# Two layers of a hybrid mixer and FFN on one core: the S5 matrices of layer 1 built beside another product, with one load per block

## The chip, the cores and the metric

One core of a Trainium2 chip. The metric is the device time of one execution in microseconds; a run counts as the time of its slowest core, which here is the only one. Five engines work from five instruction queues, each in its own order: PE (matmuls), DVE, ACT, POOL and SP (which here only starts DMAs). An instruction that waits holds back everything behind it in its queue, and a DMA is started by an instruction in the queue of SP, ACT or POOL.

## The reference

For an activation of 256 tokens by 2048 channels, two layers each compute a norm, a wide projection, three mixers (block-sparse attention, an S5 state-space mixer, a gated delta rule), an output projection, and a convolutional FFN of width 5504:

```python
for l in range(DEPTH):                                   # DEPTH = 2
    h = rmsnorm(x, attn_norm[l])
    (q, kc, vc, ks, vs, kw, vw, nsa_gates, u, qkv, z, a, b) = jnp.split(h @ w_in[l], split_points, axis=-1)
    y_a = nsa_mixer(...); y_b = s5_mixer(u, ...); y_c = gdn_mixer(...)
    x = x + concat([rmsnorm(y_a), rmsnorm(y_b), y_c]) @ w_out[l]
    x = x + conv_ffn(rmsnorm(x, ffn_norm[l]), ffn_w_in[l], ffn_conv[l], ffn_conv_b[l], ffn_w_out[l])
```

The S5 mixer is a complex linear recurrence per group. The kernel runs it four tokens at a time, and so needs, for each layer, tables of powers of the recurrence's factor and four blocks of small matrices that hold B and C multiplied by its powers. These depend on parameters alone, not on x.

## The kernel before, in words

All large products go through `product` (lines 353 to 367) or its token-major twin. A product reads its weights in units: `load` (L338) brings one unit of up to 1024 columns per partition (512 KB) into `raw` by a DMA of SP; `weight` splits it in two by `split_to`, ACT copying the high part `whi` (L327) and DVE subtracting it from `raw` to give the low part `wlo` (L328); PE then issues three matmuls per 128 rows (high by high, high by low, low by high; L295). `raw`, `whi` and `wlo` have three buffers each, so the split runs at most three units ahead of PE.

The FFN (`ffn`, from L451) runs in two halves of 22 and 21 column blocks f. In each half the first product makes, for every f, a gate and an up column block (two products of 48 matmuls, evacuated by DVE at L436, followed by a convolution on ACT and DVE at L441 and L443, a silu, a multiplication and another split into gh and gl). Then the second product makes 16 column blocks c of the output from the 22 (or 21) gh, gl: 66 (63) matmuls per c in three weight units, one addition per c on DVE (L484).

The S5 matrices of layer 1 are made during the FFN of layer 0, those of layer 0 at the start of its own mixers, by the same two functions:
- `s5_tables` (L970): some 75 tiny DVE instructions on 128x16 tiles, two sines on ACT, two powers on POOL, then POOL doubles a table `tb` six times (L1044 to L1049).
- `s5_blocks(ct)`, ct = 0 to 3 (L1054): four DMAs of 64 KB from ACT's queue bring B into `s5b` (L1066) and C straight into the block's matrix tile `s5V` (L1067); POOL multiplies B by a coefficient and then three times by the factor (helper `times`, L1075 to L1077); PE transposes eight 128x128 pieces of `s5V` (L1091), ACT copies them (`s5g`, L1094), PE multiplies small pieces of `s5V` into W, ACT copies W (L1109), and SP writes everything to a DRAM tensor `parts`, in five DMAs. `s5V`, `s5b` and `s5g` have one buffer each: the next block's first write to `s5V` waits until PE, ACT and SP have read the last one.

Order: the program is traced in source order, and a list scheduler then puts each engine's instructions in the order in which its own model of time finds them ready, with source order as priority. Nothing moves at run time. `issue_after(i)` adds an edge: every instruction traced inside it, on the engine of i, stands behind i in that engine's queue. In the kernel before, the tables of layer 1 are traced after the first product of the FFN's first half, behind the POOL power of the FFN's norm, and block ct at f = 24, 28, 32, 36 of the second half's first product.

Of the kernel before, what the change touches and what calls it, by code (L numbers as in the profile page):

```python
# [6 lines left out]
F32 = mybir.dt.float32  # L7
F32R = mybir.dt.float32r
BF16 = mybir.dt.bfloat16
AF = mybir.ActivationFunctionType  # L10
OP = mybir.AluOpType
# [25 lines left out]
SUB = 4  # L37
TABLES = (24, 28, 32, 36)
NC4 = T // SUB
# [220 lines left out]
def _s5_mats(inp, l):  # L260
    out = np.zeros((4, 2, 64, 16, 2, 16), np.float32)
    for i, nm in enumerate(("b_re", "b_im", "c_re", "c_im")):
# [3 lines left out]
        for gp in range(2):  # L266
            out[i, gp, :, :, gp] = a[:, :, gp]
    return np.ascontiguousarray(out.reshape(4, 128, 512).transpose(1, 0, 2))

# [3 lines left out]
class _K:  # L273
# [51 lines left out]
    def split_to(self, hi, lo, src, engine=None):  # L325

        self.nc.scalar.activation(out=hi, in_=src, func=AF.Copy)  # L327
        (engine or self.nc.vector).tensor_tensor(lo, src, hi.bitcast(F32), OP.subtract)  # L328

# [117 lines left out]
    def ffn(self, last):  # L447
        nc, tc = self.nc, self.tc
# [3 lines left out]
        with tc.tile_pool(name="ffn", bufs=2, reuse_waits="tile") as fp, tc.tile_pool(name="skewg", bufs=1) as skew, \  # L452
                tc.tile_pool(name="ffg", bufs=23, reuse_waits="tile") as gp:
            skew.tile([128, 16], F32, name="skewg")
            for hf, fs in enumerate(HALVES):
                gh, gl = {}, {}
                for f in fs:
                    if hf and not last and f in TABLES:
                        self.l += 1
                        self.s5_blocks(TABLES.index(f))  # L460
                        self.l -= 1
                    out = []
# [12 lines left out]
                if hf:  # L475
                    self.acc = self.squares()
                elif not last:
                    self.l += 1
                    with tc.issue_after(self.pow):
                        self.s5_tables()  # L480
                    self.l -= 1
                for c in range(16):
                    ps = self.product(("fo", hf, c), fs, gh, gl)
                    nc.vector.tensor_tensor(self.x[c], ps, self.x[c], OP.add)  # L484
                    if hf and not last:
                        self.add_square(self.acc, c)
# [566 lines left out]

    def s5_blocks(self, ct):  # L1054

        nc, s5 = self.nc, self.s5v[1]
        gt = self.either(12).tensor_tensor
        src = self.ap[f"s5m{self.l}"].rearrange("p m (t q h) -> p m t q h", t=4, q=4)[:, :, ct]

# [3 lines left out]
                               ap=[V.ap[0], [256, 8], [128 + 32 * (2 * m - 3), 2], [1, 32]])  # L1063
        sb = s5.tile([128, 4, 2, 32], F32, name="s5b", tag="s5b")
        for r in range(2):
            nc.scalar.dma_start(sb[:, :, r, :], src[:, r])  # L1066
            nc.scalar.dma_start(v6[:, :, r, 1, 0, :], src[:, 2 + r])  # L1067

        def times(out, x, by, n):
# [445 lines left out]
```

## Time and profile before

| | us |
|---|---|
| median of three runs | 2512.08 |
| the three runs | 2519.9, 2479.57, 2512.08 |
| the profiled execution, its own time | 2475.74 |
| its span, first to last instruction | 2473.9 |
| mean granted TensorE clock in it | 0.985 of full |

All durations below come from the profiled execution; its span leaves 1.8 us outside. A busy time is the sum over an engine's instructions in a stretch; "[x <-Y]" behind a row is the idle time of that engine just before the row and what ended it.

### The profile page before, as it was taken

The page shows a single profiled execution, that of the slowest core. Times are in us where ns is not written, and L with a number is a line of the kernel's source. Part 1 is how long each engine was busy: PE and PEld are TensorE (multiplying, and loading weights), DVE is VectorE, ACT ScalarE, POOL GpSimd, SP SyncE. Part 2 cuts the span into 40 slices and gives each one's busy share as a digit, 9 for nine tenths or more (in the row PEclk, how much of TensorE's full clock was granted, in tenths as well). Part 3 has the DMA queues.
Part 4 walks back from the last instruction along what each step waited for, and adds up shares of the span by engine and source line. Part 5 has one row for each costly group of instructions (what it writes and reads, how often), then busy time and mean ns, then how long its engine had stood idle before and what let it go on. Part 6 is the DMA issues. An engine that isn't in the chain of part 4 may idle for free.

```text
span 2473.9 us, 53497 instructions
## 1 busy us (share of the span) xinstructions
PE 2417.8 (98%) x21822; PEld 2338.8 (95%) x21822; DVE 1773.5 (72%) x3058; ACT 1224.7 (50%) x1911; POOL 362.8 (15%) x470
## 2 busy tenths in 40 slices
PE   8889999999999999999999999999999999999999
PEld 8879898899999999999999999988999999999999
DVE  8778766778777557787667887577877765677754
ACT  5444444564555445555545444445655544455543
POOL 7753013007100003410000021210000000000000
PEclk9999998999999999999999999989999999999999
DMA  7667455364666666666776644643655556555565
GB/s 247 174 196 206 149 183 175 98 186 159 195 195 193 191 197 206 207 208 193 213 234 202 220 138 150 216 139 99 194 195 193 193 192 196 194 194 196 193 204 175
DMA packets 206086, 463.16 MB, mean 187 GB/s; under 512 B 47600, under 2 KB 95120, under 8 KB 205840
## 3 DMA queue, kind: packets, MB, share of 16 engines
q1 hardware_dynamic: 187344, 456.13, 58.5%
q10 hardware_dynamic: 17984, 2.62, 0.6%
q8 instruction: 171, 2.80, 0.5%
q0 software_dynamic: 512, 0.98, 0.1%
q14 instruction: 75, 0.61, 0.1%
HBM read 437.96 MB, written 18.63 MB: 185 GB/s over the span
## 4 chain that ended last, share of the span: by engine, by line
PE 84%; DVE 5%; POOL 4%; DMA 3%; issue 2%; ACT 1%; ACTq 0%; SPq 0%; DVEq 0%; POOLq 0%
PE gps L295 75%; PE mpss L295 3%; PE mpsh L295 3%; PE mpsm L295 2%; DVE wlo L328 2%; POOL s5tmp L1075 2%; DMA parts<-s5g 1%; DMA raw<-w 1%; ACT whi L327 1%; DMA s5V<-s5m 1%; DVE xl L388 1%; PE mpss L907 0%; POOL s5V L1077 0%; DVE cva L443 0%; POOL s5V L1076 0%
## 5 line engine op out<-in xcount | busy, mean ns | idle before, releaser
L327 ACT ACTIVATE whi<-raw 128x1024 fp32r<-128x1024 f32 (+5 forms) x824 | 826.0, 1004 | 957.7 <-PE gps L295 804.7
L328 DVE TENSOR_TENSOR wlo<-raw,whi 128x1024 fp32r<-128x1024 f32 (+5 forms) x824 | 970.4, 1178 | 451.0 <-ACT whi L327 438.8
L295 PE MATMUL gps<-xh,wlo 128*128 128x256 f32 x3904 | 1090.6, 279 | 12.9 <-DVE wlo L328 12.7
L295 PE MATMUL gps<-xh,whi 128*128 128x256 f32 x3904 | 1090.2, 279 | 8.3 <-ACT whi L327 5.9
L295 PE MATMUL gps<-xl,whi 128*128 128x256 f32 x3904 | 1088.6, 279 | 0.0
L295 PEld LDWEIGHTS gps<-xh,wlo 128*128 128x128 f32 x3904 | 738.6, 189 | 19.2 <-DVE wlo L328 15.9
L295 PEld LDWEIGHTS gps<-xh,whi 128*128 128x128 f32 x3904 | 737.9, 189 | 12.4 <-ACT whi L327 6.7
L295 PEld LDWEIGHTS gps<-xl,whi 128*128 128x128 f32 x3904 | 738.4, 189 | 3.8 <-issue 3.0
L295 PE MATMUL gps<-gl,whi 128*128 128x256 f32 x1376 | 379.6, 276 | 0.0
L295 PE MATMUL gps<-gh,wlo 128*128 128x256 f32 x1376 | 379.6, 276 | 0.0
L295 PE MATMUL gps<-gh,whi 128*128 128x256 f32 x1376 | 379.1, 276 | 0.0
L295 PEld LDWEIGHTS gps<-gh,wlo 128*128 128x128 f32 x1376 | 258.3, 188 | 0.0
L295 PEld LDWEIGHTS gps<-gl,whi 128*128 128x128 f32 x1376 | 258.3, 188 | 0.0
L295 PEld LDWEIGHTS gps<-gh,whi 128*128 128x128 f32 x1376 | 258.0, 188 | 0.0
L295 PE MATMUL gps<-mh,wlo 128*128 128x256 f32 x512 | 148.0, 291 | 2.3 <-DVE wlo L328 2.3
L295 PE MATMUL gps<-mh,whi 128*128 128x256 f32 x512 | 148.3, 293 | 0.0
L295 PE MATMUL gps<-ml,whi 128*128 128x256 f32 x512 | 147.9, 291 | 0.0
L436 DVE TENSOR_TENSOR cvp<-gps,R 128x256 f32<-128x256 f32 x220 | 92.6, 422 | 59.9 <-PE gps L295 59.1
L295 PEld LDWEIGHTS gps<-mh,wlo 128*128 128x128 f32 x512 | 100.9, 198 | 4.2 <-DVE wlo L328 2.7
L295 PEld LDWEIGHTS gps<-ml,whi 128*128 128x128 f32 x512 | 101.2, 198 | 0.1
L295 PEld LDWEIGHTS gps<-mh,whi 128*128 128x128 f32 x512 | 100.7, 198 | 0.2
L443 DVE SCALAR_TENSOR_TENSOR cvag<-cvp,parf,cvag 128x255 f32<-128x255 f32 (+1 forms) x172 | 89.6, 521 | 5.1 <-ACT cvag L441 2.2
(358 smaller groups left out, 2534.6 us busy)
## 6 DMA issues: line engine op xcount, KB each, us to landing
raw<-w SPq DMA_DIRECT2D x572, 512.0 KB, 4.1
raw<-w SPq DMA_DIRECT2D x192, 448.0 KB, 3.9
raw<-w SPq DMA_DIRECT2D x32, 320.0 KB, 3.1
raw<-w SPq DMA_DIRECT2D x32, 256.0 KB, 2.6
s5go<-parts SPq DMA_DIRECT2D x32, 192.0 KB, 4.4
parts<-s5V SPq DMA_DIRECT2D x16, 256.0 KB, 2.9
parts<-s5g SPq DMA_DIRECT2D x16, 256.0 KB, 3.7
s5gi<-parts SPq DMA_DIRECT2D x32, 128.0 KB, 3.6
```

The costliest lines, as they stand in the source:

```text
L295: self.nc.tensor.matmul(out, lhsT, rhs, start=start, stop=stop)
L327: self.nc.scalar.activation(out=hi, in_=src, func=AF.Copy)
L328: (engine or self.nc.vector).tensor_tensor(lo, src, hi.bitcast(F32), OP.subtract)
L388: nc.vector.scalar_tensor_tensor(o, self.x[k], self.p(gain, k), h.bitcast(F32), OP.mult, OP.subtract)
L436: nc.vector.tensor_tensor(p, ps, R, OP.mult)
L443: nc.vector.scalar_tensor_tensor(a[:, j:], p[:, :T - j], tap(n - 1 - j), a[:, j:], OP.mult, OP.add)
L1075: gt(t[i], x, w.to_broadcast(shape), OP.mult)
```

## The change

The tables of layer 1 are traced in the second product of the FFN's first half, ahead of c = 1, their DVE instructions behind the low part of the last weight unit traced so far. Blocks 0 to 3 follow ahead of c = 4, 7, 10 and 13 of the same product. The host now lays the S5 inputs out so that one block's B and C stand side by side (a contiguous 1 KB of each per partition); one DMA per block brings both (256 KB) into `s5b`, which is larger and has two buffers, and for layer 1 that DMA stands in ACT's queue behind the last copy of a high part traced so far. C then goes from `s5b` into `s5V` by a copy on POOL, at the head of the block. Both layers use the new load and copy; layer 0's tables and blocks stay where they are in the source.

```diff
--- before.py
+++ after.py
@@ -35,7 +35,7 @@
 )
 BANKS = (3, 2, 2, 1)
 SUB = 4
-TABLES = (24, 28, 32, 36)
+TABLES = (1, 4, 7, 10, 13)
 NC4 = T // SUB
 BASE = 16
 SKEW = 192
@@ -265,7 +265,8 @@
         a = a.reshape(64, 16, 2, 16)
         for gp in range(2):
             out[i, gp, :, :, gp] = a[:, :, gp]
-    return np.ascontiguousarray(out.reshape(4, 128, 512).transpose(1, 0, 2))
+
+    return np.ascontiguousarray(out.reshape(2, 2, 128, 16, 32).transpose(2, 0, 3, 1, 4)).reshape(128, 2, 1024)
 
 
 
@@ -324,8 +325,10 @@
 
     def split_to(self, hi, lo, src, engine=None):
 
-        self.nc.scalar.activation(out=hi, in_=src, func=AF.Copy)
-        (engine or self.nc.vector).tensor_tensor(lo, src, hi.bitcast(F32), OP.subtract)
+        self.copied = self.nc.scalar.activation(out=hi, in_=src, func=AF.Copy).ins
+        i = (engine or self.nc.vector).tensor_tensor(lo, src, hi.bitcast(F32), OP.subtract).ins
+        if engine is None:
+            self.split = i
 
 
     def load(self, key, pool=None):
@@ -455,10 +458,6 @@
             for hf, fs in enumerate(HALVES):
                 gh, gl = {}, {}
                 for f in fs:
-                    if hf and not last and f in TABLES:
-                        self.l += 1
-                        self.s5_blocks(TABLES.index(f))
-                        self.l -= 1
                     out = []
                     for s, j in (("g", f), ("u", NF + f)):
                         ps = first or self.product(("f" + s, f), range(KT), xh, xl)
@@ -474,12 +473,15 @@
                     self.split_to(gh[f], gl[f], g)
                 if hf:
                     self.acc = self.squares()
-                elif not last:
-                    self.l += 1
-                    with tc.issue_after(self.pow):
-                        self.s5_tables()
-                    self.l -= 1
                 for c in range(16):
+                    if not hf and not last and c in TABLES:
+                        self.l += 1
+                        if c == TABLES[0]:
+                            with tc.issue_after(self.split):
+                                self.s5_tables()
+                        else:
+                            self.s5_blocks(TABLES.index(c) - 1, self.copied)
+                        self.l -= 1
                     ps = self.product(("fo", hf, c), fs, gh, gl)
                     nc.vector.tensor_tensor(self.x[c], ps, self.x[c], OP.add)
                     if hf and not last:
@@ -1051,21 +1053,25 @@
             if n < NC4:
                 pc, pq = square(pc, pq)
 
-    def s5_blocks(self, ct):
+    def s5_blocks(self, ct, after=None):
 
         nc, s5 = self.nc, self.s5v[1]
         gt = self.either(12).tensor_tensor
-        src = self.ap[f"s5m{self.l}"].rearrange("p m (t q h) -> p m t q h", t=4, q=4)[:, :, ct]
+        bc = s5.tile([128, 2, 4, 2, 32], F32, name="s5b", tag="s5b", bufs=2)
+        load = lambda: nc.scalar.dma_start(bc.rearrange("p m q r h -> p m (q r h)"),
+                                           self.ap[f"s5m{self.l}"][:, :, 256 * ct:256 * ct + 256])
+        if after is None:
+            load()
+        else:
+            with self.tc.issue_after(after):
+                load()
 
         V = s5.tile([128, 4 * 512], F32, name="s5V", tag="s5V")
         v6 = V.rearrange("p (q r b s h) -> p q r b s h", q=4, r=2, b=2, s=4)
         at = lambda m: bass.AP(tensor=V.tensor, offset=V.offset + 32 * (3 - m),
                                ap=[V.ap[0], [256, 8], [128 + 32 * (2 * m - 3), 2], [1, 32]])
-        sb = s5.tile([128, 4, 2, 32], F32, name="s5b", tag="s5b")
-        for r in range(2):
-            nc.scalar.dma_start(sb[:, :, r, :], src[:, r])
-            nc.scalar.dma_start(v6[:, :, r, 1, 0, :], src[:, 2 + r])
-
+        sb = bc[:, 0]
+        self.either(12).tensor_copy(v6[:, :, :, 1, 0, :], bc[:, 1])
         def times(out, x, by, n):
 
             shape = [128, 8, n, 32]
```

ACT's queue before, in the FFN's first product of the first half (layer 0), about twenty weight units into it; `s5b<-s5m` is a load for layer 1:

```order
L1066 DMA s5b<-s5m 128x4x32 x2
L327 ACTIVATE whi<-raw 128x1024
L441 ACTIVATE cvag<-cvp,parf 128x256
L327 ACTIVATE whi<-raw 128x1024
L469 ACTIVATE sg<-cvag 128x256
L327 ACTIVATE whi<-raw 128x1024
L441 ACTIVATE cvau<-cvp,parf 128x256
L327 ACTIVATE whi<-raw 128x1024
L327 ACTIVATE gh<-gg 128x256
L327 ACTIVATE whi<-raw 128x1024
L441 ACTIVATE cvag<-cvp,parf 128x256
L1066 DMA s5b<-s5m 128x4x32
```

ACT's queue of the change, in the second product of that half; the copies of high parts that stand between the two loads are those of c = 4 to 6:

```order
L1061 DMA s5b<-s5m 128x2x256
L328 ACTIVATE whi<-raw 128x1024
L328 ACTIVATE whi<-raw 128x896 x2
L328 ACTIVATE whi<-raw 128x1024
L328 ACTIVATE whi<-raw 128x896 x2
L328 ACTIVATE whi<-raw 128x1024
L328 ACTIVATE whi<-raw 128x896 x2
L1061 DMA s5b<-s5m 128x2x256
L1100 ACTIVATE s5g<-mpss 128x512
```

The loads have left the first product; in the second they go into a buffer that is free, and between them stand only copies of high parts.

PE's queue before, at block 0 of layer 1, in the second half's first product at f = 24:

```order
L295 MATMUL gps<-xh,whi 128x256
L295 MATMUL gps<-xl,whi 128x256
L295 MATMUL gps<-xh,wlo 128x256
L1091 MATMUL mpss<-cst,s5V 128x128 x8
L295 MATMUL gps<-xh,whi 128x256
```

PE's queue of the change, at the same transposes:

```order
L296 MATMUL gps<-gh,whi 128x256
L1097 MATMUL mpss<-cst,s5V 128x128 x4
L296 MATMUL gps<-gl,whi 128x256
L296 MATMUL gps<-gh,wlo 128x256
L1097 MATMUL mpss<-cst,s5V 128x128 x4
```

Here 418 of the second product's 1056 matmuls stand ahead of the first transposes (6.33 c). Those of blocks 1, 2 and 3 stand at 8.76, 11.35 and 14.52 c, and the small matmuls into W, the last PE reads of `s5V`, 0.33 c behind the transposes.

DVE's queue before, in the tables, in the first product; `s5ps` and `s5pc` hold the factors of `tb`'s doublings, and POOL's first doubling waits for the pair that these rows make:

```order
L328 TENSOR_TENSOR wlo<-raw,whi 128x1024
L1021 TENSOR_TENSOR s5pc_10470<-s5pc_10470,s5t 128x16
L443 SCALAR_TENSOR_TENSOR cvag<-cvp,parf,cvag 128x255
L1018 TENSOR_TENSOR s5t<-s5ps_10471 128x16
L1019 TENSOR_TENSOR s5t_10469<-s5pc_10470,s5ps_10471 128x16
L1020 TENSOR_TENSOR s5pc_10472<-s5pc_10470 128x16
L443 SCALAR_TENSOR_TENSOR cvag<-cvp,parf,cvag 128x254
L1022 TENSOR_SCALAR s5ps_10473<-s5t_10469 128x16
```

DVE's queue of the change, at the same steps; the low part that leads is that of the first weight unit of c = 2:

```order
L329 TENSOR_TENSOR wlo<-raw,whi 128x1024
L1012 COPY s5c_10545<-s5ci 128x32
L1023 TENSOR_TENSOR s5pc_10548<-s5pc_10548,s5t 128x16
L1020 TENSOR_TENSOR s5t<-s5ps_10549 128x16
L1021 TENSOR_TENSOR s5t_10547<-s5pc_10548,s5ps_10549 128x16
L1022 TENSOR_TENSOR s5pc_10550<-s5pc_10548 128x16
L1024 TENSOR_SCALAR s5ps_10551<-s5t_10547 128x16
```

The same steps have moved from between convolutions to behind a split for the second product.

## Rows read from the trace of the kernel before

**Rows 1.** The page: part 1's engine totals, and part 4's chain by engine.

```profile
PE 2417.8 (98%) x21822; PEld 2338.8 (95%) x21822; DVE 1773.5 (72%) x3058; ACT 1224.7 (50%) x1911; POOL 362.8 (15%) x470
...
PE 84%; DVE 5%; POOL 4%; DMA 3%; issue 2%; ACT 1%; ACTq 0%; SPq 0%; DVEq 0%; POOLq 0%
```

**Rows 2.** Windows, FFN of layer 0: length; busy PE, PEld, DVE, ACT, POOL; clock; DMA.

```profile
581.34:630.79 49.45, 43.20 (x338) 42.20 (x337) 42.38 (x64) 20.94 (x29) 42.95 (x50) 0.93 0.54 161
630.79:641.70 10.91, 10.91 (x98) 10.91 (x98) 8.27 (x12) 5.79 (x9) 0.00 (x0) 1.00 0.68 210
836.86:844.34 7.48, 7.48 (x68) 7.48 (x67) 3.83 (x4) 2.97 (x4) 0.00 (x0) 1.00 0.58 198
940.91:949.00 8.09, 8.09 (x106) 7.81 (x105) 4.61 (x8) 4.89 (x10) 2.45 (x3) 1.00 0.77 217
940.91:1091.92 151.01, 148.40 (x1426) 146.17 (x1425) 120.46 (x151) 82.69 (x121) 56.65 (x52) 1.00 0.68 208
...
605.00:610.00 5.00, 3.25 (x15) 3.05 (x16) 4.09 (x6) 3.67 (x6) 4.90 (x5) 0.68 0.43 115
```

**Rows 3.** Timeline of ACT: start, length, instruction, idle time before it. ACTq is its queue.

```profile
603.69 0.98 ACTq L1066 DMA_DIRECT2D s5b<-s5m  x2
604.79 1.06 ACT L327 ACTIVATE whi<-raw 128x1024 fp32r<-128x1024 f32 x1 [4.91 <-PE gps L295]
...
624.02 1.06 ACT L327 ACTIVATE whi<-raw 128x1024 fp32r<-128x1024 f32 x1 [5.35 <-POOL s5tmp L1075]
...
966.11 0.60 ACT L441 ACTIVATE cvag<-cvp,parf 128x256 f32<-128x256 f32 x1 [4.25 <-POOL s5tmp L1075]
```

**Rows 4.** Timeline of PE behind those two ACT waits.

```profile
605.90 0.39 PE L295 MATMUL gps<-xh,whi 128*128 128x256 f32 x1 [1.65 <-ACT whi L327]
...
625.13 0.38 PE L295 MATMUL gps<-xh,whi 128*128 128x256 f32 x1 [2.85 <-ACT whi L327]
```

**Rows 5.** Timelines of POOL and of DVE: tables and block 0 of layer 1.

```profile
579.33 0.22 POOL L1045 TENSOR_TENSOR s5tmp<-tb,s5ps 128x16 f32<-128x16 f32 x1 [12.22 <-DVE s5pc L1021]
...
602.29 1.37 POOL L1075 TENSOR_TENSOR s5tmp<-s5b,s5c 128x256 f32<-128x256 f32 x2
...
604.84 1.27 POOL L1049 TENSOR_TENSOR tb<-tb,s5tmp 128x512 f32<-128x512 f32 x1
...
614.33 3.09 POOL L1075 TENSOR_TENSOR s5tmp<-s5V,s5l 128x512 f32<-128x512 f32 x2
...
622.31 1.18 POOL L1075 TENSOR_TENSOR s5tmp<-s5b,s5c 128x256 f32<-128x256 f32 x2
623.46 0.72 POOL L1076 TENSOR_TENSOR s5V<-s5tmp 128x256 f32<-128x256 f32 x1
...
579.07 0.16 DVE L1021 TENSOR_TENSOR s5pc<-s5pc,s5t 128x16 f32<-128x16 f32 x1
```

**Rows 6.** Groups by line and shape: POOL up to 170 us, then the FFN's second product.

```profile
L1310 POOL COPY ub<-cst 32x256 f32<-32x256 f32 x1 | 0.7, 736 | 0.0
L1098 POOL MEMSET s5W<- 128x512 f32 x4 | 2.1, 522 | 1.5 <-DMA parts<-s5W 1.5
...
L328 DVE TENSOR_TENSOR wlo<-raw,whi 128x1024 fp32r<-128x1024 f32 x24 | 29.4, 1225 | 31.6 <-ACT whi L327 31.5
L327 ACT ACTIVATE whi<-raw 128x1024 fp32r<-128x1024 f32 x24 | 25.5, 1063 | 38.2 <-PE gps L295 38.2
```

**Rows 7.** Timelines of the start of layer 0: PE, then ACT, then POOL.

```profile
88.81 1.11 PE L1091 MATMUL mpss<-cst,s5V 128*128 128x128 f32 x4 [3.49 <-POOL s5V L1076]
...
118.64 1.11 PE L1091 MATMUL mpss<-cst,s5V 128*128 128x128 f32 x4 [1.42 <-POOL s5V L1076]
...
68.94 0.51 ACT L439 ACTIVATE cva<-cvp,parm 128x256 f32<-128x256 f32 x1 [2.26 <-issue]
...
102.15 3.02 POOL L1075 TENSOR_TENSOR s5tmp<-s5V,s5l 128x512 f32<-128x512 f32 x2 [3.83 <-DMA s5V<-s5m]
107.54 2.04 POOL L1075 TENSOR_TENSOR s5tmp<-s5V,s5l 128x512 f32<-128x512 f32 x2
```

## The prediction, made before the run

> **What bounds the kernel now.** I read the page first. PE is busy 98% of the span and the chain that ended last runs 84% through it [rows 1], so a change can win only where PE stands still or runs below its rate, and loses wherever it adds a wait to PE. Next come the windows, to see what PE's rate is. With POOL idle, two products of the FFN of layer 0 take 10.91 us, 5.455 each, and one column block c of the second product takes 7.48 us, with PE busy throughout and its clock at 1.00 [rows 2]. These are the rates against which stretches with POOL at work are held.
>
> The first such stretch, 581.34 to 630.79, holds POOL's tables and block 0 for layer 1 beside seven products. Seven take 38.2 us at the rate; the stretch has 49.45 [rows 2]. So 11.3 us are lost, of which PE's idle time is 49.45 - 43.20 = 6.25. The timelines name the cause. ACT stands still for 4.91 and 5.35 us with a load of `s5b` at the head of its queue, until POOL has read the one buffer [rows 3]; behind the load wait copies of high parts, and PE waits for those, 1.65 and 2.85 us before the copy alone [rows 4]. The remaining 5.05 us beyond the idle time, 2.5 per stall, are slow running after it: at 605 to 610 the granted clock is 0.68 of full, a mean of the levels 1.2 and 2.4 GHz, right behind an idle PE [rows 2].
>
> The second stretch, 940.91 to 1091.92, holds the PE part of block 0 and all of blocks 1 to 3 beside 25 products: 136.4 us at the rate. The PE work of one block shows alone in 940.91 to 949.00: 8.09 - 5.455 = 2.6 us; four make 10.5. The stretch took 151.01, so 4.1 us are lost [rows 2], again with a load waiting in ACT's queue, 4.25 us behind POOL's reading of the B before it [rows 3].
>
> **The change, part by part.** *Loads of layer 1.* They leave both stretches, and what they meet in the second product is a free buffer and copies around them. The ACT stalls on `s5b` go, and DVE, 86% busy in the first stretch (42.38 of 49.45) with POOL's instructions beside it, is relieved [rows 2]. I take back all that was lost: 11.3 + 4.1 = 15.4 us. The upper bound is that sum; the lower is the second stall's part alone, some 5 us, if the rest came from the tables' DVE work rather than the loads. I take the upper end because each loss ends in a row that names the load's release [rows 3, 4].
>
> *Tables and blocks in the second product.* PE's own 2.6 us per block move and cost the same. DVE is only 51% busy there (3.83 of 7.48) [rows 2], so I cost the 75 small DVE instructions at nothing: the split is up to three units ahead. Without that cover they would cost up to what the first stretch lost beyond the load stalls.
>
> The term that decides is a new wait: PE's transposes of block 0 stand 6.33 c into the product, that is 47.3 us behind its start, and PE stops there until POOL has the matrices. When has it? POOL's doublings need factors that DVE makes behind the split of the first unit of c = 2. Its buffer comes free when PE ends the first unit of c = 1: 7.48 + 24 of 66 matmuls, 2.72, makes 10.2 us. Add the copy, 1.06, the split, 1.23 [rows 6], and six small DVE instructions of at most 0.16 [rows 5], 0.8 with their overlap: POOL starts at 13.3. In the trace the tables then take 26.8 us (579.33 to 606.11), and block 0 from there to the end of its last L1076, without the 1.18 us for the next block's B, 16.9 [rows 5]. Those are beside a DVE 86% busy. The same pair of L1075 took 3.09 us there and 2.04 us in a calmer place [rows 5, 7], a ratio of 0.66. So the bounds are 17.7 and 26.8 for the tables, 11.2 and 16.9 for the block. For a DVE 51% busy I go that share of the way between them: 23.1 and 14.6. The new copy of C on POOL is of a kind that the trace has not; the nearest row, a COPY of the same columns, took 0.74 us [rows 6]. Its bounds are 0.5, the memset row [rows 6], and 1.4, a pair of half-size multiplications (602.29) [rows 5]. POOL is ready at 13.3 + 23.1 + 0.7 + 14.6 = 51.7, and PE waits 4.4 us. With all low bounds (42.9) it waits nothing, with all high ones (58.4) 11.1. To a wait belongs the slow running behind it, 2.5 us as above. Behind the waiting PE stand further matmuls, ACT's copy of the transposes with the next high parts, and SP's writes with the next raw loads; all wait for the same event, so nothing is added.
>
> Blocks 1 to 3: `s5V` comes free 0.33 c and 2.6 us behind the transposes, 5.1 us; POOL then needs copy, memset and block, 0.7 + 0.5 + 14.6. That loop of 20.9 us stands against 2.43 c + 2.6 = 20.8 on PE's side for block 1, 22.0 for block 2, 26.3 for block 3. I take 0.1 us.
>
> The Trainium skill, SBUF — State Buffer, section Who interferes with whom, has a DVE instruction with two SBUF inputs hold off a GpSimd instruction that reads SBUF, for its whole length. The L1075 pairs, 3.09 against 2.04 us, agree in kind. By that rule taken strictly, three splits of some 1.15 us per c would leave POOL 54% of the time, and tables and block would take longer than in the first stretch, not shorter; the saturated first stretch itself [rows 2, 5] does not bear out so strict a reading, which is why its durations are my upper bound.
>
> *Loads and copy in layer 0.* PE waits 3.49 us for block 0's matrices and 1.42 us for block 1's, and ACT stood 2.26 us around a load; POOL waits 3.83 us per block for C behind the release of `s5V` [rows 7], where now a copy of 0.7 us stands, since the load came earlier. In the changed order the transposes of block 0 stand 13 matmuls later, 1.5 us. Gains: 1.5 for block 0, 1.4 for block 1, about 1 of ACT's 2.26: 4 us. Bounds: 7.2, the sum of the three waits, and a loss of 3, four copies in POOL's way in a stage where DVE and DMA also end waits.
>
> The sum: -15.4 + 4.4 + 2.5 + 0.1 - 4 = -12.4, rounded to -12 us. Against the profiled execution's 2475.7 (span 2473.9 and 1.8 outside) that is 2464. The median of the runs shown is 2512.1, 1.5% above the profiled execution, and the three runs lie at 2480 and at 2512 to 2520; the sum doesn't depend on which. I set the same 12 us against the median: 2500 us.
>
> **The rivals.** Rival A, POOL in time: POOL falls near its low bounds and PE never waits. For it: DVE has half its time free. Against: the schedule puts the transposes where its own model finds them ready, and as I read the ACT waits, POOL ran 4.91, 5.35 and 4.25 us behind that model [rows 3]. Price: -15.4 - 4 = -19.4, 2456 profiled, 2493 at the median.
>
> Rival B, the other side: POOL is as slow as beside the saturated DVE, and PE waits at block after block. With 26.8 and 16.9 the first wait is 13.3 + 26.8 + 0.7 + 16.9 - 47.3 = 10.4; the loop is 23.2, so 2.4 for block 1 and 1.2 for block 2; three stalls add 7.5. That is 21.5 against 15.4: +6, and +6 only if layer 0 gives nothing: 2482 profiled, 2518 at the median. It decides once the waits pass 15.4 less 2.5 per stall. The skill's rule above stands behind it. For it: the lag rows [rows 3]; against it: 51% against 86%.
>
> Rival C, a trade: the load stalls go, but one wait of 10.4 + 2.5 us takes their place and layer 0 stays as it is. -15.4 + 12.9 = -2.5: 2473 profiled, 2510 at the median.
>
> Rival D: the loads still block. A load of the change waits for POOL's read of the block two before; with two buffers and a block's length between them no row supports it. Nothing comes back then, and the moved waits are added: +3 to +7, in price like B.
>
> **How the numbers follow.** Forecast 0.50, A 0.18, C 0.17, B 0.12, D 0.03. The forecast's own range is -5 to -17 us. The cases run from -19 to +6, so at the upper level of the runs 2493 to 2518; a median at the lower level would read 2456 to 2482. The range 2458 to 2518 takes in both and leaves out the ends. What a measurement of this kernel can tell from no change is about 2%, 50 us; no case comes near. Only a median that changes level besides, with A's gain, gets there: faster 0.05, same 0.93, slower 0.02.
>
> **What would show it.** Right: no ACT wait on POOL's L1075 counterpart in the first half's first product, and a steady 5.4 to 5.5 us per product where 49.45 us went for seven; 25 products of the second half at the rate; one PE wait for `s5V` of 2 to 8 us about 47 us into the second product, with a lower clock behind it, and small ones after. Wrong: a wait at each block of over 2 us (B), none (A), a load in ACT's queue with an ACT wait before it (D), or time lost in layer 0's first 200 us.

## The result, and the profile after

The changed kernel is slower, by less than 1%. Its median is 2506.35 us (22 runs, 2487.20 to 2534.73), that of the kernel before 2487.60 us (22 runs, 2473.13 to 2519.90). The ratio is 1.0066, 95% interval 1.0043 to 1.0088. The profiled execution took 2494.25 us against 2475.74: 18.5 us more.

The stages tell where they went. Their borders are the additions into `x` on DVE (L486 after, L484 before): layer 0's mixers end with the last of theirs; the FFN's first product (first half) lasts from there to the first addition of the second product; the second product from its first to its last addition; the second half from there to its own last addition. Where PE is busy throughout, a window of 25 us shows either 223 or 215 matmuls (granted clock 1.00 at both), and a stage at 215 is 1.039 times as long; the column "rate" is that of the second half. Each ratio leaves out the runs over 1.5% above the fastest of their kernel, two of e4_mixq's six among them; the traces of e1_ahead and e2_home are of such runs, and that of e3_again is of a single one.

| kernel | layer 0's mixers | first product | second product | second half | rate | ratio to before (95%) |
|---|---|---|---|---|---|---|
| before | 544.3 | 263.1 | 112.2 | 357.7 | 223 | 1 |
| changed | 550.9 | 247.9 | 152.9 | 342.7 | 223 | 1.0066 (1.0043 to 1.0088) |
| changed, second trace | 545.2 | 247.7 | 150.9 | 342.6 | 223 | one run |
| e1_load | 545.2 | 251.3 | 112.2 | 390.5 | 215 from 1075 | 1.0087 (1.0047 to 1.0126) |
| e1_move | 541.5 | 249.6 | 153.1 | 356.1 | 215 | 1.0040 (1.0001 to 1.0079) |
| e1_zero | 545.3 | 248.1 | 150.5 | 356.2 | 215 | 1.0043 (1.0002 to 1.0084) |
| e1_ahead | 546.1 | 256.9 | 147.5 | 356.2 | 215 throughout | 1.0064 (1.0031 to 1.0096) |
| e2_home | 550.9 | 259.7 | 118.3 | 376.7 | 215 from 625 | 1.0017 (0.9977 to 1.0057) |
| e2_both | 541.1 | 247.7 | 140.5 | 342.3 | 223 | 1.0052 (1.0013 to 1.0092) |
| e2_late | 551.8 | 248.4 | 141.3 | 363.9 | 215 | 1.0124 (1.0070 to 1.0179) |
| e2_bothlate | 545.2 | 247.5 | 136.4 | 356.2 | 215 | 1.0043 (1.0001 to 1.0085) |
| e3_mix | 549.8 | 247.6 | 122.0 | 370.1 | 223 | 1.0051 (1.0015 to 1.0088) |
| e3_mixold | 546.5 | 247.7 | 122.0 | 369.5 | 223 | 1.0062 (1.0026 to 1.0098) |
| e4_q | 538.4 | 247.3 | 147.3 | 342.7 | 223 | 1.0034 (0.9996 to 1.0072) |
| e4_mixq | 541.5 | 256.9 | 116.3 | 366.6 | 215 throughout | 0.9881 (0.9824 to 0.9939) |
| e4_lateq | 540.1 | 248.1 | 133.7 | 342.7 | 223 | 0.9929 (0.9887 to 0.9971) |
| e5_baseq | 545.4 | 262.9 | 112.2 | 370.4 | 215 from 1100 | 1.0021 (0.9991 to 1.0052) |

In the changed kernel the first product gains 15.2 and the second half 15.0, of which 10.5 is PE work that moved; the second product takes 40.7 more, 30.2 beyond that work; layer 0's mixers 6.6 more; layer 1 1.5 more. -15.2 - 4.5 + 30.2 + 6.6 + 1.5 = 18.6.

The page's totals, and its chain by engine, where POOL has 6% in place of 4% [rows 1]:

```profile
PE 2421.3 (97%) x21822; PEld 2339.9 (94%) x21822; DVE 1749.8 (70%) x3058; ACT 1225.0 (49%) x1911; POOL 360.9 (14%) x478
...
PE 83%; POOL 6%; DMA 4%; DVE 4%; issue 1%; ACT 1%; SPq 0%; ACTq 0%; DVEq 0%; POOLq 0%
```

Windows of the changed kernel (columns as in [rows 2]). The first product is now full; in the second, 800 to 950, PE loses 8.5, 7.4 and 6.4 us, and its clock is below 1.00 in each:

```profile
600.00:650.00 50.00, 50.00 (x443) 50.00 (x443) 37.34 (x55) 27.42 (x37) 0.00 (x0) 1.00 0.65 192
800.00:850.00 50.00, 41.53 (x353) 41.34 (x352) 28.28 (x61) 16.41 (x17) 43.72 (x56) 0.91 0.58 173
850.00:900.00 50.00, 42.56 (x428) 41.41 (x427) 19.80 (x20) 18.54 (x24) 33.25 (x34) 0.98 0.62 191
900.00:950.00 50.00, 43.62 (x410) 42.87 (x411) 18.02 (x18) 17.34 (x23) 21.34 (x22) 0.88 0.64 187
950.00:1000.00 50.00, 50.00 (x444) 50.00 (x443) 36.99 (x52) 25.73 (x34) 0.00 (x0) 1.00 0.66 199
```

The timeline of PE at the transposes of blocks 0 to 3: one wait of the forecast's kind at each block, not at the first alone.

```profile
846.46 1.12 PE L1097 MATMUL mpss<-cst,s5V 128*128 128x128 f32 x4 [8.46 <-POOL s5V L1082]
...
872.12 0.66 PE L1097 MATMUL mpss<-cst,s5V 128*128 128x128 f32 x4 [2.09 <-POOL s5V L1082]
...
901.76 1.12 PE L1097 MATMUL mpss<-cst,s5V 128*128 128x128 f32 x4 [6.69 <-POOL s5V L1082]
...
935.38 1.11 PE L1097 MATMUL mpss<-cst,s5V 128*128 128x128 f32 x4 [4.62 <-POOL s5V L1082]
```

The timeline of POOL says why: the tables begin at 803.96; then each block from 1 on is held, by the release of `s5V` (5.50), by its load (7.48), and by the memset of `s5W`, which waits until the write of the block before has landed (4.74, 14.04).

```profile
803.96 0.23 POOL L1047 TENSOR_TENSOR s5tmp<-tb,s5ps 128x16 f32<-128x16 f32 x1 [8.27 <-DVE s5pc L1023]
...
832.14 1.44 POOL L1082 TENSOR_TENSOR s5V<-s5tmp 128x128 f32<-128x128 f32 x1
...
845.68 0.72 POOL L1082 TENSOR_TENSOR s5V<-s5tmp 128x256 f32<-128x256 f32 x1
...
853.74 0.40 POOL L1074 COPY s5V<-s5b 128x256 f32<-128x256 f32 x1 [5.50 <-PE mpss L296]
...
880.23 0.62 POOL L1081 TENSOR_TENSOR s5tmp<-s5b,s5c 128x256 f32<-128x256 f32 x1 [7.48 <-DMA s5b<-s5m]
...
887.48 0.53 POOL L1104 MEMSET s5W<- 128x512 f32 x1 [4.74 <-DMA parts<-s5W]
...
916.42 0.53 POOL L1104 MEMSET s5W<- 128x512 f32 x1 [14.04 <-DMA parts<-s5W]
```

The waits grouped (total, times, longest): the first four rows are from 785 on (POOL's from 795) to 950, the last three from the first 300 us, layer 0. SP, which issues the loads of the weights in order, stands for POOL's `s5V` and ACT's `s5g` ahead of the writes of `parts`:

```profile
PE mpss L1097 <- POOL s5V L1082: 21.9, 4, 8.5
...
POOL s5W L1104 <- DMA parts<-s5W: 18.8, 2, 14.0
...
SPq L1094 <- POOL s5V L1082: 32.6, 4, 10.9
SPq L1101 <- ACT s5g L1100: 18.1, 5, 5.5
...
PE mpss L1097 <- POOL s5V L1082: 13.9, 3, 5.0
...
POOL s5W L1104 <- DMA parts<-s5W: 11.1, 3, 6.3
...
SPq L1094 <- POOL s5V L1082: 16.9, 3, 8.4
```

### The profile page after: what moved, and what is told of

It is laid out like the page before. It is cut to its first block, busy times and chain, and to the rows that moved or that the text cites. A ratio compares the mean times of both kernels' runs of the same rounds, so it can differ in the third digit from the quotient of the medians.

```text
span 2492.4 us, 53461 instructions
## 1 busy us (share of the span) xinstructions
PE 2421.3 (97%) x21822; PEld 2339.9 (94%) x21822; DVE 1749.8 (70%) x3058; ACT 1225.0 (49%) x1911; POOL 360.9 (14%) x478
## 4 chain that ended last, share of the span: by engine, by line
PE 83%; POOL 6%; DMA 4%; DVE 4%; issue 1%; ACT 1%; SPq 0%; ACTq 0%; DVEq 0%; POOLq 0%
PE gps L296 73%; PE mpss L296 3%; PE mpsh L296 3%; PE mpsm L296 2%; POOL s5tmp L1081 2%; DVE wlo L329 2%; DMA raw<-w 1%; DMA parts<-s5g 1%; POOL s5V L1082 1%; POOL s5V L1083 1%; ACT whi L328 1%; PE mpss L909 1%; DMA parts<-s5W 0%; DVE cva L446 0%; POOL s5tmp L1047 0%
## 5 line engine op out<-in xcount | busy, mean ns | idle before, releaser
L296 PEld LDWEIGHTS gps<-xh,wlo 128*128 128x128 f32 x3904 | 736.0, 189 | 10.6 <-DVE wlo L329 7.9
L446 DVE SCALAR_TENSOR_TENSOR cvag<-cvp,parf,cvag 128x255 f32<-128x255 f32 (+1 forms) x172 | 82.7, 481 | 3.0
```

Source lines behind the costliest of these rows:

```text
L296: self.nc.tensor.matmul(out, lhsT, rhs, start=start, stop=stop)
L446: nc.vector.scalar_tensor_tensor(a[:, j:], p[:, :T - j], tap(n - 1 - j), a[:, j:], OP.mult, OP.add)
```

## The experiments

**The change in two.** e1_load keeps the places of the kernel before and has the new loads; e1_move keeps the old loads and has the new places.

```diff
-TABLES = (1, 4, 7, 10, 13)
+TABLES = (24, 28, 32, 36)
...
+                    if hf and not last and f in TABLES:
...
+                        self.s5_blocks(TABLES.index(f), self.copied)
```

> The loads alone: one load per block, two buffers, behind ACT's copies, with tables and blocks left where the kernel before has them (tables behind the pow, blocks ahead of products 24, 28, 32, 36 of the second half). Theory 1 (the loads were right, the move is what cost): the 11.3 us of 581 to 631 and the 4.1 of 941 to 1092 come back, layer 0 gives or takes 3, so 12 to 18 us below before, ratio 0.993 to 0.995. Theory 2 (the new load costs in layer 0 what it saves in the FFN): layer 0 some 8 to 12 us longer by 250 us, ratio 0.998 to 1.002.

> The move alone: tables and blocks ahead of c = 1, 4, 7, 10, 13 of the first half's second product, with the four loads per block and the single buffer of the kernel before. Theory 1 (the move costs): the second product of the first half loses 25 to 40 us against its rate, less the 10.5 us of PE work and the 4.1 of stalls that leave the second half and the 7 or more that leave the first half's first product: 5 to 20 us above before, ratio 1.002 to 1.008, and layer 0 as before. Theory 2 (the move is neutral, the new load or its copy is what cost): within 3 us of before or below it.

e1_load came out at 1.0087, against both theories. The first product did gain 11.8 (263.1 to 251.3), and layer 0 is within 1 us of before; the loss is in the second half, 390.5, of which some 8 are its rate from 1075 on (224 us less 224 / 1.039). There each load, queued behind the last copy traced so far, lands late for its own block, and PE waits 18.8 us. Timeline of POOL and waits of PE in its second half:

```profile
970.95 0.53 POOL L1105 MEMSET s5W<- 128x512 f32 x1 [12.58 <-DMA parts<-s5W]
990.34 0.91 POOL L1075 COPY s5V<-s5b 128x256 f32<-128x256 f32 x1 [18.86 <-DMA s5b<-s5m]
...
PE mpss L1098 <- POOL s5V L1083: 18.8, 4, 6.4
```

e1_move's ratio, 1.0040, lies in the band of its first theory. It took 153.1 for the second product, as much as with both parts: the move costs there whichever load it has. Its second half ran at 215; at 223 it would be the changed kernel's 342.7.

**What holds POOL.** e1_zero clears `s5W` once per layer; e1_ahead issues the load of block n + 1 when block n is queued.

```diff
-        W = s5.tile([128, 4, 4, 32], F32, name="s5W", tag="s5W")
-        self.either(12).memset(W, 0.0)
+        if ct == 0:
+            self.W = s5.tile([128, 4, 4, 32], F32, name="s5W", tag="s5W")
+            self.either(12).memset(self.W, 0.0)
+        W = self.W
```

```diff
+        if ct == 0:
+            self.s5_load(0, after)
+        if ct < 3:
+            self.s5_load(ct + 1, after)
+        bc = self.bc.pop(ct)
```

> The changed kernel with W's tile allocated and cleared once per layer instead of once per block (its zeros are never written). Theory 1 (POOL held at the memset by SP's write of the block before): POOL's waits for parts<-s5W, 18.8 us in the second product and 11.1 in layer 0, are gone; block 2 ready some 5 us and block 3 some 18 us earlier; PE's waits for s5V fall from 35.8 to 20 or less in all; 10 to 20 us below the changed kernel, ratio to before 0.998 to 1.003. Theory 2 (POOL is slow at the blocks by itself, beside DVE): the wait only turns into one for the tile V's release by PE, and the time stays within 3 us of the changed kernel, ratio 1.005 to 1.008.

> The changed kernel with each block's load issued when the block before it is queued, so that block 2's load no longer stands between ACT's two copies of block 1. Theory 1 (the memset of W sets block 2's time, as it waits for a write that lands at 887.5 whatever the load does): the 7.5 us wait on s5b<-s5m goes, the wait for parts<-s5W in block 2 grows by as much, and the time stays within 3 us of the changed kernel, ratio 1.005 to 1.008. Theory 2 (the load behind ACT's copies sets it): 6 to 9 us below the changed kernel, ratio 1.002 to 1.004.

e1_zero: 150.5 us for the second product, and PE's waits for `s5V` fall from 21.9 to 18.0 only. What the memset no longer holds, late loads hold, 21.8 us of POOL's waits where it was 7.5:

```profile
POOL s5V L1074 <- DMA s5b<-s5m: 13.7, 1, 13.7
...
POOL s5tmp L1081 <- DMA s5b<-s5m: 8.1, 1, 8.1
```

e1_ahead: 147.5 us at 215, where the 122.7 of PE's work are 127.5; 20.0 beyond the work in place of 30.2, and PE's waits at 15.8. My account of it, that the memset would hold POOL as long, fell: as block 2 came earlier, W's write came earlier with it, and what POOL then waits for above all is the release of `s5V`:

```profile
POOL s5V L1082 <- PE mpss L296: 17.7, 3, 6.6
...
POOL s5W L1112 <- DMA parts<-s5W: 6.1, 3, 2.5
```

So the load is the larger gate, the memset stands behind it. In the times neither shows: both ratios' intervals hold the changed kernel's 1.0066. The traces, single executions, are read here for their waits; which kernel is faster only the ratios say.

**Both gates, and the places.** e2_both has both edits, with the first two loads issued with the tables. e2_late moves the blocks alone, to c = 5, 9, 12, 15. e2_bothlate has both edits and c = 7, 10, 13, 15. e2_home has both edits and the places of the kernel before. The diff is that of e2_bothlate, without the two edits shown above.

```diff
-TABLES = (1, 4, 7, 10, 13)
+TABLES = (1, 7, 10, 13, 15)
...
                             with tc.issue_after(self.split):
                                 self.s5_tables()
+                            self.s5_load(0, self.copied)
+                            self.s5_load(1, self.copied)
```

> The loads without their lateness, in the places of the kernel before: the first two loads are issued with the tables, each other one when the block before it is queued, and W is cleared once per layer. Theory 1 (the loads' size is right, their place behind ACT's copy at the block itself is what made PE wait 18.8 us for s5V in the second half with the loads alone): those four waits fall under 4 us in all, the second half of the first FFN takes 350 to 356 us where every dense stretch is at 223 matmuls per 25 us (357.7 before, 390.5 with the loads alone), the time 8 to 16 us below before, ratio 0.993 to 0.997. Theory 2 (the new load and the copy cost POOL and ACT as much as they save wherever they stand): PE still waits 10 us or more at the blocks, ratio 1.000 or above.

> The changed kernel with both of block 2's and block 3's gates taken away: W cleared once per layer, and loads issued a block ahead; blocks where the change has them. Theory 1 (memset and late load stood behind each other, so that taking one alone left the other): no POOL wait for parts<-s5W or s5b<-s5m in the second product, POOL waits for V's release alone; PE's waits for s5V there fall from 21.9 us to 10 to 14 (8 of them at block 0, where POOL is not ready), 8 to 12 us below the changed kernel, ratio 1.000 to 1.003. Theory 2 (V's release by PE, one buffer, sets the pace of the blocks): the waits stay at 17 us or more, ratio 1.004 to 1.007.

> The changed kernel with the blocks ahead of c = 5, 9, 12, 15 in place of 4, 7, 10, 13, loads and memset as changed; by the order the transposes of blocks 1 to 3 come 1.8, 2.2 and 2.0 products later. Theory 1 (the gates cost, and later blocks do not open them as they follow PE's own transposes of the block before): PE still waits 12 to 20 us for s5V, ratio 1.003 to 1.007. Theory 2 (the blocks only stood too close for POOL): waits of 8 us or less, ratio 0.997 to 1.002.

> Both gates taken away and the blocks ahead of c = 7, 10, 13, 15; by the order block 0's transposes come 0.7 of a product later than in the changed kernel (7.0 against 6.3), the others at 10.0, 13.0 and 15.4. Theory 1 (POOL's lead and V's release are what is left): block 0 waits 3 to 5 us in place of 8.5, the others 0 to 3 each, 5 to 12 in all; the second product takes 134 to 142 us in place of 152.9; ratio 0.994 to 0.999, below before. Theory 2 (beside the second product the blocks cost PE as much in any place): the second product stays above 146 us, ratio 1.003 or above.

e2_both: 140.5 us for the second product, 12.4 below the changed kernel, and PE's waits down to 10.7, of which 8.7 are at block 0 and 2.0 at the other three. No wait of POOL for the memset or a load is left; the two gates together were worth that in the trace. Waits of PE, then of POOL:

```profile
PE mpss L1108 <- POOL s5V L1093: 10.2, 3, 8.7
...
PE mpss L1108 <- POOL s5V L1094: 0.5, 1, 0.5
...
POOL s5V L1085 <- PE mpss L296: 12.2, 2, 7.2
POOL s5tmp L1050 <- DVE s5pc L1026: 7.7, 1, 7.7
POOL s5V L1085 <- DMA parts<-s5V: 4.9, 1, 4.9
```

Its ratio, 1.0052, is above the expected band and inside that of the second theory, with an interval that reaches from 1.0013 to 1.0092: the waits speak for the first theory, the time does not yet. e2_late: PE still waited 16.8 us, and one block's PE work slid into the second half (363.9); later places alone don't open the gates. Its ratio, 1.0124 from four runs, is above its band too. e2_bothlate: 136.4, with 5.8 us of waits for `s5V`, as expected; but its ratio, 1.0043, misses the 0.994 to 0.999 of its first theory, so no ratio yet shows a kernel below the one before. e2_home: PE never waits for `s5V` in the second half, so the late load and the memset together explained those waits of e1_load; yet its second half took 376.7 where 353.2 x 1.039 = 367.0 would be without a stall, its ratio, 1.0017, misses the 0.993 to 0.997, and what PE waits for are now the weights' parts:

```profile
PE gps L296 <- ACT whi L328: 5.2, 2, 2.9
PE gps L296 <- DVE wlo L329: 3.1, 4, 1.0
```

**A mixture, layer 0, and a second trace.** e3_mix leaves tables and first loads in the second product (ahead of c = 1) and puts the blocks back into the second half, with both edits. e3_mixold gives layer 0 the four old loads. e3_again is the changed kernel, unedited.

```diff
-                    if not hf and not last and c in TABLES:
+                    if not hf and not last and c == 1:
...
+                    if hf and not last and f in TABLES:
...
+                        self.s5_blocks(TABLES.index(f), self.copied)
```

```diff
+        else:
+            sb = s5.tile([128, 4, 2, 32], F32, name="s5b", tag="s5b")
...
+                nc.scalar.dma_start(sb[:, :, r, :], src[:, 0, :, r])
+                nc.scalar.dma_start(v6[:, :, r, 1, 0, :], src[:, 1, :, r])
```

> Only the tables and the first two loads in the second product (ahead of c = 1), the blocks back ahead of products 24, 28, 32, 36 of the second half, loads a block ahead, W cleared once per layer. Theory 1 (the change was right in taking tables and loads out of the first product, wrong in putting the blocks closer than POOL and V's one buffer allow): with every dense stretch at 223 matmuls per 25 us, the first product takes 247 to 249 us (263.1 before), the second product 112 to 114, the second half 353 to 356 (357.7 before): 15 to 19 us below before, layer 0's 0 to 5 off that; ratio 0.993 to 0.997. Theory 2 (loads and copy cost the same wherever they stand, or layer 0 eats it all): ratio 1.000 or above.

> The same, with layer 0's loads as before: four per block, half of them straight into V, no copy on POOL. Theory 1 (the new load costs layer 0 some 4 us, by the copy on POOL, which is late there, and by a load that waits in ACT's queue for POOL): layer 0 ends at 541 to 545 us in place of 545 to 551, ratio 0.002 below that of the run with the new loads. Theory 2 (layer 0's end moves with PE's rate and the clock, not with the loads): both end alike, within 3 us, and the ratios agree within 0.001.

> The changed kernel once more, nothing edited, for a second trace. Theory 1 (PE's dense rate, 223 or 215 matmuls per 25 us at a granted clock of 1.00, is drawn anew after a stretch with stalls, whatever the kernel): the stages with stalls take the same time as in the first trace within 3 us, and a dense stretch (the second half, 342.7 us) may come out at 356. Theory 2 (the rate is fixed by the kernel's order): every dense stretch has the rate of the first trace.

e3_mix was no gain: the first product as expected, but 122.0 for the second and 370.1 for the second half, though PE waits for `s5V` nowhere in either. Timelines of SP, then of ACT, then a window show it. SP issues one raw load at 833.78 and then stands until POOL's `s5V` lets the next row, a write, go at 847.23; the loads behind it come late, ACT waits 12.26 us for `raw`, and PE loses 7 of 20 us at a clock of 0.74:

```profile
833.78 0.33 SPq L341 DMA_DIRECT2D raw<-w  x1
847.23 1.06 SPq L1106 DMA_DIRECT2D parts<-s5V  x2
...
839.15 0.95 ACT L328 ACTIVATE whi<-raw 128x896 fp32r<-128x896 f32 x1 [1.32 <-PE gps L296]
852.37 0.95 ACT L328 ACTIVATE whi<-raw 128x896 fp32r<-128x896 f32 x1 [12.26 <-DMA raw<-w]
...
840.00:860.00 20.00, 13.01 (x90) 12.52 (x89) 6.16 (x7) 4.01 (x5) 7.72 (x9) 0.74 0.51 160
```

e3_mixold ends layer 0 at 546.5 against 549.8, and its ratio is no lower: that the load itself costs layer 0 some 4 us is not borne out. e3_again bears out its first theory for the rate, though the rate changed in layer 1 and not in the second half; its rows are in the last section. Its layer 0 ended 5.7 us earlier, where the theory allowed 3.

**SP's queue.** e4_q, e4_mixq and e4_lateq take the writes of `parts` out of SP's queue, in the changed kernel, in e3_mix and in e2_bothlate; e5_baseq does so in the kernel before.

```diff
-            nc.sync.dma_start(rows(384 + 128 * r, 128), v6...
+            nc.gpsimd.dma_start(rows(384 + 128 * r, 128), v6...
...
-            nc.sync.dma_start(rows(128 * r, 128), g...
+            nc.scalar.dma_start(rows(128 * r, 128), g...
...
-        nc.sync.dma_start(rows(256, 128), W...
+        nc.scalar.dma_start(rows(256, 128), W...
```

> The changed kernel with the writes of parts taken out of SP's queue: s5V's from POOL's queue, s5g's and s5W's from ACT's, where the engine that makes the tile issues its write. Theory 1 (SP waits for POOL and ACT ahead of those writes and the weights wait behind SP): SP's waits on s5V and s5g, 50.7 us in the second product, are gone, ACT waits for raw less than 3 us there, the second product takes 140 to 147 us in place of 152.9 (PE still waits for s5V), ratio 1.001 to 1.005. Theory 2 (the time beside the waits is the clock after them, and SP's wait only runs beside PE's): the second product stays at 149 to 153 us, ratio 1.006 or above.

> Tables and first loads in the second product, blocks back in the second half, loads a block ahead, W cleared once, and the writes of parts out of SP's queue. Theory 1 (SP's queue held the weights): the second product takes 112 to 115 us (122.0 with the writes in SP's queue), the second half 352 to 358 (370.1), in dense stretches at 223 per 25 us; 10 to 18 us below before in a trace with fast stretches only, ratio 0.993 to 0.998. Theory 2 (ACT's own queue and copies make the weights late): 119 us or more and 365 or more, ratio 1.002 or above.

> Blocks ahead of c = 7, 10, 13, 15 of the second product, loads ahead, W cleared once, and the writes of parts out of SP's queue. Theory 1: the second product takes 126 to 132 us in place of 136.4 (122.7 without any stall), ratio 0.994 to 0.999. Theory 2 (POOL's lead and V's one buffer alone): 134 us or more, ratio 1.002 or above.

> The kernel before with the writes of parts out of SP's queue and nothing else. Theory 1 (the gain is the sum of both: layer 0 gains 3 to 6 from SP's queue, the first product's 15 and the second half's 4 need the loads and tables moved): layer 0 ends at 538 to 542 (544.3 before), the first product stays at 260 to 264 and the second half at 355 to 358; ratio 0.996 to 1.000, above that of e4_mixq. Theory 2 (SP's queue was all of it, the ACT stalls on s5b were beside it): the first product falls to 250 or less, ratio 0.986 to 0.992.

e4_mixq beats both kernels: 0.9881, a larger gain than expected. The ratio rests on four of its six runs; the median of all six is 2469.85 us against 2482.40 for the kernel before beside it, and the mean of all six is 0.993 of that kernel's. Its profiled execution ran at 215 in this FFN, where 112.2 without a stall is 116.6, and 342.7 + 10.5 = 353.2 is 367.0; it took 116.3 and 366.6. So in the second product and the second half nothing is left to hide. The windows where e3_mix lost 7 us are full:

```profile
820.00:840.00 20.00, 20.00 (x173) 20.00 (x171) 12.32 (x11) 7.63 (x8) 19.75 (x17) 1.00 0.60 193
840.00:860.00 20.00, 20.00 (x172) 20.00 (x171) 11.87 (x11) 7.45 (x9) 12.06 (x11) 1.00 0.70 221
```

e4_lateq also gains, 0.9929, with 133.7 for the second product: the time is above the band of its first theory, as PE still waits 6.3 us once for `s5V`. e4_q: 147.3, 5.6 less than the changed kernel, at the edge of its band; its ratio, 1.0034, is not clear of the changed kernel's 1.0066. Layer 0 ends at 538.4, where SP no longer waits for `s5V` or `s5g`. e5_baseq gains nothing, 1.0021, and its first product stays at 262.9: the free queue helps only together with tables and loads moved. It also misses its first theory in layer 0, which ends at 545.4 where 538 to 542 was expected: the queue alone does not bring the 538.4 of e4_q.

The Trainium skill, DMA: Bandwidth & Descriptors, section Issuing engines are not separate DMA queues, holds that issuing from several engines saves only the sequencer's time to start a transfer. In the rows of e3_mix SP's starts take 0.33 and 0.53 us each, and what another issuing engine saved there was more: the wait of transfers queued behind one whose data wasn't ready, for which ACT stood 12.26 us.

## Why the prediction was wrong, step by step

**Loads leave both stretches, -15.4: right in kind, small.** 15.2 in the first product and 15.0 - 10.5 = 4.5 in the second half came back, 19.7. The first product gave 3.9 more than the window of [rows 2] showed; e1_load got 11.8 of its 15.2 by the loads alone.

**The lead of POOL, a wait of 4.4: right in kind, half the size.** POOL began 803.96 - 790.66 = 13.3 us into the product (DVE takes the last `fu` product at 790.66), as forecast. From there to 832.14 are 28.2 us, 27.8 without the copy's 0.40, where 23.1 + 0.7 were forecast. The block took 14.3 (14.6 forecast). PE waited 8.46.

What failed is the scaling by DVE's busy share (its 23.1 and 14.6 stand 51/86 of the way between the bounds; 51% of the way would be 22.3 and 14.1). DVE was 71% busy beside the tables, which it helps to make, and 26% beside the block, where PE's wait had stopped the splits: that the block came out as forecast is luck. By the rows, POOL pays for each split it meets. Timelines of POOL and of DVE, then the two windows:

```profile
821.58 1.90 POOL L1047 TENSOR_TENSOR s5tmp<-tb,s5ps 128x512 f32<-128x512 f32 x1
823.44 1.05 POOL L1049 TENSOR_TENSOR tb<-tb,s5pc 128x512 f32<-128x512 f32 x1
...
821.45 1.12 DVE L329 TENSOR_TENSOR wlo<-raw,whi 128x896 fp32r<-128x896 f32 x1 [0.41 <-ACT whi L328]
...
803.96:832.14 28.18, 28.18 (x251) 28.18 (x250) 20.08 (x41) 11.06 (x12) 28.10 (x39) 1.00 0.66 200
832.14:846.40 14.26, 5.85 (x52) 5.65 (x50) 3.73 (x4) 1.91 (x2) 13.77 (x16) 0.80 0.38 117
```

In the tables eleven POOL instructions ran beside a split and took 0.84 to 1.11 us longer than the shortest of their shape in the two traces, 10.3 us in all. In the tables of the kernel before there were seven, 7.1 us; in block 0 of the change three, 2.8 us; in block 1 seven, 6.5 us. The second product has three splits in 7.48 us, the first product two in 5.455: for POOL the new place is no calmer. No run moved the splits, so this is read from rows alone.

The rule of the Trainium skill, SBUF — State Buffer, section Who interferes with whom, agrees with these rows: the eleven shared 0.97 to 1.41 us each with splits and lost 0.84 to 1.11. Read strictly, it had the tables slower than in the first stretch, and they were, 27.8 against 26.8; the block's 14.3 against 16.9 does not speak against it, as that block met only three splits.

**Blocks 1 to 3, 0.1 us: the step that failed.** "POOL then needs copy, memset and block" took the release of `s5V` as the only gate. Measured: waits of 2.09, 6.69 and 4.62, and with block 0's, 152.9 - 122.7 - 21.9 = 8.3 us of slow running, 2.1 for each of four stalls (2.5 forecast, for one). Two gates were missed, at blocks 2 and 3: the memset waits for the write of W, which SP issues, and the load of block 2 stood in ACT's queue between the two copies of block 1's transposes. In the kernel before, with layer 1's blocks four column blocks f (eight products) apart, the memset waited only in layer 0, 1.5 us [rows 6]. Block 1 met neither gate. There the loop itself was mis-sized: `s5V` came free 7.3 us behind the first transposes (5.1 forecast) and POOL took 18.4 us (15.8), 6.5 of them beside splits, against 23.6 on PE's side (20.8). With both gates away (e2_both) the three waits sum to 2.0 us in place of 13.4, and the second product is 12.4 us shorter, in one trace each; the ratios, 1.0052 and 1.0066, don't tell these two kernels apart.

**"SP's writes with the next raw loads; all wait for the same event, so nothing is added": failed.** e3_mix loses 9.8 us in the second product with no wait of PE for `s5V`, and moving the writes alone gave it all back. Of the missed steps this is the one that the ratios show too: 1.0051 (1.0015 to 1.0088) became 0.9881 (0.9824 to 0.9939), and in the second pair, e2_bothlate and e4_lateq, 1.0043 (1.0001 to 1.0085) became 0.9929 (0.9887 to 0.9971).

**Layer 0, -4: no gain shows.** 6.6 more in one trace, 0.9 in the other. PE's waits for `s5V` there are 13.9 and 9.2 us where the kernel before had 7.4; the memset waits 11.1 where it waited 1.5 [rows 6]. The four traces with the new loads and no further edit there (the changed kernel twice, e1_load, e2_late) end the stage at 545.2 to 551.8, the two with layer 0 as before (e1_move is the other) at 544.3 and 541.5. With the writes out of SP's queue PE's waits fall to 6.5 in e4_q, and the stage to 538.4, 541.5 and 540.1 in the three traces, but e5_baseq, with that queue and the old loads, has 545.4. The stage moves by 5.7 us between two executions of one kernel, so the size of this term and its cause stay open.

**The sum.** -12.4 was forecast and 18.6 measured. Of the 31.0 us between them 19.1 are in blocks 1 to 3 and the slow running, 10.6 in layer 0 (4.9 by the second trace), 4.1 in the lead and 1.5 in layer 1; the loads took 4.3 off.

**Rivals.** B came nearest: a wait at each block. Its first wait was priced 10.4 (8.46), the others 3.6 together (13.4), the clock 7.5 (8.3); its sum, +6, fell short by the two missed gates and layer 0. That the median, 2506, came within 6 us of the 2500 forecast is luck: the 12 us were taken from 2512, the median of three runs, and 22 runs of the kernel before have 2488. The difference is within the 2% that had nearly all the chance.

## What to carry to other kernels

Before work is moved into a denser place, list every gate of the engine that carries it, buffers that only a slow write frees (even for a memset) and loads that stand in another engine's queue, and take the last of them as the loop. A write whose data comes from a slow engine does not belong in the queue that feeds the weights: issue it from the engine that makes the data. Price POOL beside DVE by the splits that it will meet, not by DVE's busy share. When one gate is taken away and nothing moves, look for a second behind it before dropping the theory.

## What the runs showed of the hardware

PE, busy throughout and at a granted clock of 1.00, has two rates in these traces: 223 or 215 matmuls of 256 columns per 25 us. The changed kernel shows both with nothing edited. Windows of its second trace, then of its first:

```profile
1000.00:1100.00 100.00, 100.00 (x884) 100.00 (x884) 76.33 (x112) 54.52 (x74) 0.00 (x0) 1.00 0.62 194
...
2000.00:2100.00 100.00, 100.00 (x852) 100.00 (x851) 57.47 (x72) 42.82 (x50) 0.00 (x0) 1.00 0.55 184
```

```profile
2000.00:2100.00 100.00, 100.00 (x885) 100.00 (x884) 58.78 (x72) 44.61 (x52) 0.00 (x0) 1.00 0.62 192
```

In the FFNs of all these traces the rate held through each dense stretch and changed only across a stretch in which PE had stalled. It is worth 13.5 us in the second half of an FFN (342.7 to 356.2), as much as the effects studied here, so a stage was judged by its time at its rate and a kernel by many runs. What sets the rate was not tried, nor whether more stalls bring the lower one more often: of the nine traces that came at 223 to a second product with the blocks in it, five went on behind it at 223 and four at 215.
